# Grouped-query attention on one core: the order of all engines, planned by a search at build time, is replaced by an order written as a string

## The chip, the core and the metric

The kernel runs on one core of a Trainium2 chip. The metric is device time in microseconds (us) for one execution, the median of several. The core has five engines that each work through a list of instructions in order: TensorE (PE, matrix multiplication into PSUM), ScalarE (ACT), VectorE (DVE), GpSimd (POOL) and SyncE (SP, here only a queue of transfers). They wait for one another on semaphores. GpSimd works on SBUF alone; the scores lie in PSUM, where ScalarE and VectorE can read them.

## The reference: what is computed

```python
scores = scale * np.matmul(q_group, k_group.transpose(0, 1, 3, 2))
scores_max = np.max(scores, axis=-1, keepdims=True)
attn = np.exp(scores - scores_max)
attn = attn / (np.sum(attn, axis=-1, keepdims=True) + 1e-08)
output[:, q_start:q_end, :, :] = np.matmul(attn, v_group)
```

There are 8 batches, 8 query heads and 2 key/value heads (four query heads share one), 1024 positions and 64 values per head, in fp32. The scores are small, so the kernel leaves the maximum out: it takes exp(scale * score), multiplies by v with a column of ones appended, and divides by the sum that this column gives.

## The kernel before, in words

There are 64 jobs j, one for each batch and query head. A job has 8 tiles of scores ("pairs"), each 128 x 1024 in fp32, in one of three PSUM slots (`sp0` to `sp2`). A pair takes two score matmuls (L880) and then an exponential, in one of two ways:

- ScalarE: one ACTIVATE (L890) writes the pair as bf16 into `pt`.
- VectorE, by bit arithmetic: a "pass" (L901, `yt<-sp`) turns the scores into 16-bit integers whose bits are nearly those of a bf16 exponential. Two pairs make a chain, which takes three more steps in SBUF on 2048 columns: `zh` (L908, keeps the mantissa bits), `two` (L915, keeps the exponent bits, `et`) and `mul` (L924, `zt` = `yt` x `zt`). Both `et` and `zt` are then multiplied by v and added up in PSUM. The last four jobs add them on VectorE instead (L929).

GpSimd takes columns of `mul` off VectorE (L854). It does this in windows in which VectorE reads PSUM: the pass, the reciprocal of the sums (`rec`, L1007) and the normalization (`norm`, L1016). Each such multiplication is tied by a wait to the VectorE instruction just before the window.

TensorE multiplies by v in pieces of 128 rows (L942) into two PSUM banks; seven pieces fill a bank, which VectorE then normalizes into `ost`, from where SP stores it. The last job's pieces are done as its pairs become ready (L982). Dummy matmuls (L727) fill some of TensorE's idle time.

The inputs q, k and v are cast to bf16 by transfers that GpSimd issues into DRAM buffers, one for each tensor (L625); SP transposes, copies and stores.

The order of all this comes from `class Plan`, plain Python that runs when the kernel is built. It keeps a clock for each engine and advances the one that is earliest. Its constants (`M_...`) are durations in ns. For TensorE, `choices` says what could be next and which is preferred: `A` (scores for ScalarE), `D` (scores for VectorE), `V` (a few matmuls by v), `E` and `L` (pieces of the first and last job), `F` (a dummy), `W` (wait); `cost` plays each of them 7 us on and the best is taken. `quota` fixes how many pairs of a job go to VectorE. `dve` picks VectorE's next step by fixed keys. `gpsimd` is called as VectorE begins a window and gives one chain at most as many columns as fit: the window plus `M_GOVER` = 60 ns, in steps of 32 columns, at least 192. GpSimd's transfers are not in the plan: they are put behind multiplications afterwards, by the `room` that is left there. In the plan VectorE's steps take the same time whether or not GpSimd works beside them.

The plan's events, sorted by time, are then written out as instructions. From there each engine follows its list.

Of the kernel before, what the change touches and what calls it, by code (L numbers as in the profile page):

```python
# [10 lines left out]
M_START = 5450  # L11
# [6 lines left out]
M_FILL = 1e9  # L18
M_IDLE = 250
# [16 lines left out]
M_GP = 800  # L36
# [3 lines left out]
M_GOVER = 60  # L40
M_GLATE = 900
M_NORM = 531
M_HOLD = 1500
M_SPARE = 800
M_ISSUE = 900
M_LATE = 8500

M_GAP = 90
M_RUNWAY = 2100
M_BACK = 4100  # L50
M_WAIT = 250
M_TOL = 200

HORIZON = 7000
W_A = 1.0
W_D = 0.28
W_P = 0.02
W_LAG = 0
# [4 lines left out]
MXD = 2  # L63
MORE = 4
TAIL = 4
CHN = 2
SOON = 0
AHEAD = 3
LAST = ()
LONG = 6  # L70
FIRST = (2, 2, 1)
GWINS = 2
GFROM = 2
GTO = 5
GMIN = 192
GSTEP = 32
STEPS = (("zh", M_D4), ("two", M_D4), ("mul", M_D2), ("add", M_D2))


class Chain:  # L80
# [12 lines left out]
    def copy(self):  # L93
        c = Chain.__new__(Chain)
        c.__dict__.update(self.__dict__)
        c.pairs = self.pairs[:]
        return c

    def left(self):
        n = len(self.pairs)  # L100
        return sum(
            M_FIX + (self.share() if k == "mul" else 1024 * n) * r
            for k, r in STEPS[self.at : self.nsteps]
        )

    def share(self):

        return max(0, self.cols - 500 * max(0, GWINS - self.wins)) if self.nsteps == 3 else self.cols


class State:
    LISTS = "nxt dcount pcnt pmax a_of mms slot aq dq out norms lastp firstp twice".split()

    def copy(self):
        c = State.__new__(State)
        c.__dict__.update(self.__dict__)
        for k in self.LISTS:
            setattr(c, k, getattr(self, k)[:])
        new = {}

        def twin(ch):
            if ch is None:
                return None
            if ch.id not in new:
                new[ch.id] = ch.copy()
            return new[ch.id]

        c.chains = [twin(x) for x in self.chains]
        c.open = twin(self.open)
        c.heads = {k: v[:] for k, v in self.heads.items()}  # L130
        c.ev = None
        return c

    def note(self, *e):
        if self.ev is not None:
            self.ev.append(e)


class Plan:
# [5 lines left out]
    def __init__(self, nj, npt, nct, nyt):  # L145
# [9 lines left out]
        self.quota = [FIRST[j] if j < len(FIRST) else MXD + (j % MORE == MORE // 2) for j in range(nj)]  # L155
        self.quota[nj - len(LAST) :] = LAST
# [14 lines left out]
        s.tG = M_START + 9000  # L171
# [9 lines left out]
        s.ev = []  # L181
        self.run(s)
# [16 lines left out]
    def act(self, s):  # L199
        t = s.tA  # L200
        if not s.aq:
            s.tA = max(t, s.tP) + 1
        elif s.aq[0][0] > t:
            s.tA = s.aq[0][0]
        else:
            _, sl, j, c = s.aq.pop(0)
            s.note(t, "act", sl, j, c)
            s.idleA += t - s.endA
            s.tA = s.endA = t + M_ACT
            s.slot[sl] = s.tA + M_ATAIL + M_SEE  # L210
            self.ready(s, j, c, s.slot[sl])

    def gpsimd(self, s, t, window):


        at = max(t, s.tG)
        until = t + window + M_GOVER
        at += M_GLEAD
        for ch in s.chains:
# [7 lines left out]
            if ch.cols - w < GMIN:  # L227
                w = ch.cols
# [4 lines left out]
            s.note(t, "gmul", None, ch.id, (ch.cols, w))  # L233
            s.tG = at = at + M_GFIX + w * M_GCOL
            ch.parts += 1
            self.part(s, ch, s.tG + M_SEE + M_GLATE)
            break

    def dve(self, s):
        t, nj, end = s.tD, self.nj, None  # L240
        norm = s.norms and s.norms[0][0] <= t
        rec = norm and s.norms[0][1] == "rec"
        soon = s.dq and s.dq[0][0] <= t + (M_REC if rec else 0)
        if rec:
            _, _, lo, hi = s.norms[0]
            if soon:
                self.gpsimd(s, t, M_REC + 1134 + M_NORM)
                s.host = True
            s.note(t, "rec", (lo, hi), None, None)
# [3 lines left out]
        elif s.dq and s.dq[0][0] <= t and not (  # L253
            (norm and t - s.norms[0][0] > M_HOLD)
            or any(ch.pairs[0][0] < SOON for ch in s.chains)
        ):
# [15 lines left out]
            if not s.host:  # L272
                self.gpsimd(s, t, 1134 + (M_NORM if norm else 0))
            s.host = False
            s.follow = bool(norm)
            s.note(t, "dpass", sl, (ch.id, len(ch.pairs) - 1), (j, c))
# [3 lines left out]
            if len(ch.pairs) == (2 if j < LONG or j >= nj - 6 else CHN):  # L280
                s.chains.append(ch)
                s.open = None
        else:
            best = None
            if norm:
                late = s.dlast == s.norms[0][2]
                key = -1 if s.follow or s.norms[0][2] < NPIECE else 5 if late or s.dq else 0
                best = (late and key >= 0, key, None)
            for ch in s.chains:

                late = s.dlast == (ch.id, ch.at) and ch.at in (0, 3)
                first = (3, 4, 2, 1)[ch.at]
                if ch.at == 2 and ch.nsteps == 3 and ch.cols and ch.wins < GWINS:
                    if GFROM <= ch.pairs[0][0] < nj - GTO:
                        if s.dq and s.dq[0][0] < t + M_SPARE:
                            continue
                        first = 6
                key = (late, first, ch)
                if best is None or key[:2] < best[:2]:
                    best = key  # L300
            s.follow = False
            if best:
                at = max(t, s.dend + M_DEP) if best[0] else t
                ch = best[2]
                if ch is None:
                    _, _, lo, hi = s.norms.pop(0)
                    s.note(t, "norm", (lo, hi), None, None)
                    end = at + M_FIX + 64 * (hi - lo) * M_D1
                    s.out[self.group_of[lo] % 2] = end + M_DTAIL + M_SEE
                    s.dlast = None  # L310
                    s.end = s.pc == self.last and not s.left and not s.norms
                else:
                    n = len(ch.pairs)
                    kind, rate = STEPS[ch.at]
                    cols = ch.cols if kind == "mul" else 1024 * n
                    end = at
                    if cols:
                        s.note(t, kind, None, ch.id, n, cols)
                        end = at + M_FIX + cols * rate
                    if kind == "zh":  # L320
                        ch.zend = end + M_DTAIL + M_SEE
                    ch.at += 1
                    s.dlast = (ch.id, ch.at)
                    if ch.at == ch.nsteps:
                        s.chains.remove(ch)
                        self.part(s, ch, end + M_DTAIL + M_SEE)
        if end:
            s.idleD += t - s.endD
            s.tD = s.endD = end
            s.dend = end + M_DTAIL  # L330
        else:
            s.tD = max(t, s.tP) + 1
            for q in (s.dq, s.norms):
                if q:
                    s.tD = min(s.tD, q[0][0])
            s.tD = max(s.tD, t + 1)

    def pick_d(self, s):
        for j in range(s.a, min(self.nj, s.a + AHEAD)):
            if s.nxt[j] < 8 and s.dcount[j] < self.quota[j] and self.qready[j] <= s.tP:  # L340
                return j
        return None

    def choices(self, s):

        t, nj = s.tP, self.nj  # L350
        while s.a < nj and s.nxt[s.a] == 8:
            s.a += 1
        a = s.a
        cold = 2 if t < M_WARM else 1
        free = [x for x in (0, 1, 2) if s.slot[x] <= t]
        runway = s.tA - t + M_ACT * len(s.aq)
        slack = runway - cold * M_PAIR - M_PTAIL - (M_SWITCH if s.mode != "s" else 0)
        can_a = a < nj and len(s.aq) < 2 and self.qready[a] <= t and s.used_p < self.npt
        dj = None
        held = len(s.chains)  # L360
        if not s.dq and held < self.nyt and (s.open or s.used_c < self.nct):
            if max(s.tD - t, 0) + sum(ch.left() for ch in s.chains) < M_BACK:
                dj = self.pick_d(s)
        s.free, s.dj = free, dj
        can = []
        kind = None
        if free:
            can += ["A"] * can_a + ["D"] * (dj is not None)
            if dj is not None:
                if not can_a:  # L370
                    kind = "D"
                elif len(free) > 1 or slack <= M_GAP or s.mode == "s":
                    other = min(s.slot[x] for x in (0, 1, 2) if x != free[0])
                    late = not s.aq and other > s.tA - M_PAIR - M_PTAIL + M_TOL
                    kind = "A" if late or slack <= M_PAIR else "D"
# [679 lines left out]
```

## Time and profile before

The median of the three runs shown is 357.17 us (356.17 to 357.32). One execution was profiled.

| | |
|---|---|
| profiled execution | 356.55 us |
| its span, first to last instruction on the engines | 354.8 us |
| granted TensorE clock | 1.00 |
| ScalarE: exponentials (L890) | 372, 342.1 us busy |
| VectorE: passes (L901) | 140, 170.7 us |
| VectorE: `zh`, `two`, `mul` | 71 each; 47.9, 47.2 and 54.2 us |
| VectorE: `rec`, `norm` | 74 each; 73 of them 14.6 and 44.8 us |
| GpSimd: multiplications (L854) | 107, 131.9 us |
| GpSimd: transfers issued (L625) | 33 of q, 8 of k, 8 of v; 28.7 us |

In the costliest groups, "x" is the number of instructions, then come the engine's busy time in the group and the mean duration of one in ns, then the engine's idle time just before them and what ended most of it. Consecutive instructions of an engine overlap in the records, so a pass that lasts 1.22 us is followed by the next instruction after some 1.13. In the timeline a row begins with its start and its length in us.

### The profile page before, as it was taken

To read this page: it belongs to the slowest core of one execution; us is meant where nothing else is said; L and a number is where in the kernel's file an instruction comes from. 1 tells how busy PE (TensorE), PEld (TensorE's weight loads), DVE (VectorE), ACT (ScalarE), POOL (GpSimd) and SP (SyncE) were. 2 spreads that over 40 slices of the span, in tenths; PEclk is the share of its full clock that TensorE was granted. 3 is DMA by queue.
4 is the path that set the end of the run, shared out by engine and by line. 5 is a ranking of instruction groups with operands and counts; after the bars stand their busy time and mean duration, and the time that the engine had idled before them with its cause. 6 is when DMAs were issued, how large, how long until landed. Compare 5 with 4: busy or idle time off the path is not lost.

```text
span 354.8 us, 14070 instructions
## 1 busy us (share of the span) xinstructions
PE 346.3 (98%) x6236; PEld 223.1 (63%) x6236; DVE 345.3 (97%) x516; ACT 344.6 (97%) x376; POOL 160.6 (45%) x164
## 2 busy tenths in 40 slices
PE   8899999999999999999999999999999999999995
PEld 3556666666666666666666666666666666666665
DVE  4999999999999999999999999999999999999995
ACT  5999999999999999999999999999999999999993
POOL 3145554664355444563465645265543625570000
PEclk9999999999999999999999999999999999999999
DMA  6688555996675976496566976759675798556133
GB/s 159 123 134 160 127 106 124 132 151 126 131 137 117 135 141 120 84 181 157 105 95 133 164 136 132 137 84 173 135 93 124 119 174 125 122 91 126 29 91 120
DMA packets 96430, 44.82 MB, mean 126 GB/s; under 512 B 61153, under 2 KB 95073, under 8 KB 95585
## 3 DMA queue, kind: packets, MB, share of 16 engines
q1 hardware_dynamic: 94128, 31.48, 43.6%
q0 software_dynamic: 2096, 12.19, 23.9%
q8 instruction: 48, 0.79, 1.0%
q10 hardware_dynamic: 144, 0.26, 0.2%
q14 instruction: 14, 0.11, 0.1%
HBM read 27.13 MB, written 28.97 MB: 158 GB/s over the span
## 4 chain that ended last, share of the span: by engine, by line
ACT 70%; PE 24%; DVE 4%; issue 1%
ACT pt L890 70%; PE ops L942 12%; PE sp L880 10%; DVE yt L901 2%; PE ops L727 1%; DVE zt L924 1%; PE sp L982 1%; DVE zt L908 1%; DVE ost L1016 0%; DVE et L915 0%; PE sp L750 0%; PE ops L762 0%; PE ops L750 0%; DVE rec L1007 0%; DVE warm L619 0%
## 5 line engine op out<-in xcount | busy, mean ns | idle before, releaser
L890 ACT ACTIVATE pt<-sp 128x1024 bf16<-128x1024 f32 x372 | 342.1, 1039 | 0.7 <-PE sp L880 0.6
L854 POOL TENSOR_TENSOR zt<-yt,zt 128x448 bf16<-128x448 bf16 (+2 forms) x107 | 131.9, 1233 | 145.0 <-DVE et L915 45.3
L880 PE MATMUL sp<-qt,kt 64*128 64x512 bf16 x1024 | 172.7, 383 | 2.9 <-DVE yt L901 1.4
L942 PE MATMUL ops<-va,pt 128*128 128x65 bf16 x2872 | 175.3, 194 | 0.0
L901 DVE TENSOR_SCALAR yt<-sp 128x1024 uint16<-128x1024 f32 x140 | 170.7, 1219 | 0.8 <-PE sp L880 0.8
L942 PEld LDWEIGHTS <-pt 128*128 128x128 bf16 x2872 | 127.7, 97 | 33.4 <-issue 33.4
L942 PE MATMUL ops<-va,zt 128*128 128x65 bf16 x1096 | 127.7, 194 | 0.0
L942 PE MATMUL ops<-va,et 128*128 128x65 bf16 x1048 | 118.0, 194 | 0.0
L942 PEld LDWEIGHTS <-zt 128*128 128x128 bf16 x1096 | 87.5, 97 | 13.8 <-issue 13.1
L942 PEld LDWEIGHTS <-et 128*128 128x128 bf16 x1048 | 82.3, 98 | 17.6 <-issue 17.6
L880 PEld LDWEIGHTS <-kt 64*128 64x128 bf16 x1024 | 48.5, 93 | 55.9 <-issue 33.8
L924 DVE TENSOR_TENSOR zt<-yt,zt 128x896 bf16<-128x896 bf16 (+9 forms) x71 | 54.2, 763 | 0.0
L908 DVE TENSOR_SCALAR zt<-yt 128x2048 uint16<-128x2048 uint16 (+1 forms) x71 | 47.9, 675 | 0.2
L915 DVE TENSOR_SCALAR et<-yt 128x2048 uint16<-128x2048 uint16 (+1 forms) x71 | 47.2, 670 | 0.0
L1016 DVE TENSOR_TENSOR ost<-ops,rec 128x448 f32<-128x448 f32 (+2 forms) x73 | 44.8, 613 | 0.1
L625 POOL DMA_DIRECT2D qd<-in_q_dram x33 | 19.5, 592 | 4.8 <-PE sp L880 4.0
L1007 DVE RECIPROCAL rec<-ops 128x7 f32<-128x7 f32 (+2 forms) x73 | 14.6, 200 | 0.0
L727 PE MATMUL ops<-warm 128*128 128x128 bf16 (+1 forms) x36 | 5.7, 296 | 1.7 <-DVE warm L619 1.2
L625 POOL DMA_DIRECT2D kd<-in_k_dram x8 | 4.5, 560 | 5.0 <-PE sp L880 5.0
L727 PEld LDWEIGHTS <-warm 128*128 128x128 bf16 x36 | 2.8, 109 | 4.9 <-issue 3.7
L625 POOL DMA_DIRECT2D vd<-in_v_dram x8 | 4.7, 583 | 0.6 <-PE sp L880 0.6
L929 DVE TENSOR_TENSOR zt<-et,zt 128x2048 bf16<-128x2048 bf16 (+1 forms) x4 | 4.3, 1078 | 0.0
(38 smaller groups left out, 25.1 us busy)
## 6 DMA issues: line engine op xcount, KB each, us to landing
out_dram<-ost SPq DMA_DIRECT2D x64, 256.0 KB, 3.4
qd<-in_q_dram POOLq DMA_DIRECT2D x29, 256.0 KB, 4.8
kt<-kt SPq DMA_DIRECT2D x30, 64.0 KB, 3.6
va<-vd SPq DMA_DIRECT2D x30, 64.0 KB, 3.9
kd<-in_k_dram POOLq DMA_DIRECT2D x7, 256.0 KB, 4.2
vd<-in_v_dram POOLq DMA_DIRECT2D x7, 256.0 KB, 5.3
qt<-qd SPq DMA_TRANSPOSE x63, 4.0
qd<-in_q_dram POOLq DMA_DIRECT2D x5, 128.0 KB, 3.8
```

Source lines behind the costliest of these rows:

```text
L625: return nc.gpsimd.dma_start(out=t.rearrange("(a x) d -> a (x d)", a=128), in_=src.rearrange("(a x) d -> a (x d)", a=128),)
L727: nc.tensor.matmul(ops[bank][:, lo : lo + cols], lhsT=warm[:, 0:128], rhs=warm[:, 0:cols], start=not beside, stop=True, skip_group_check=b ...
L854: gps = nc.gpsimd.tensor_tensor(out=z, in0=flat(yt[j])[:, lo : lo + w], in1=z, op=ALU.mult)
L880: now = nc.tensor.matmul(sps[x][:, half, :], lhsT=t[lo : lo + D, c // NH, ci % NH * 128 : (ci % NH + 1) * 128], rhs=qt[j][lo : lo + D, 0, ...
L890: exps.append(nc.scalar.activation(out=p, in_=where_s[(j, c)], func=AF.Exp, scale=scale))
L901: vec = nc.vector.tensor_scalar(out=yt[ch][:, i, :, :], in0=where_s[c], scalar1=EXP_A, scalar2=EXP_B, op0=ALU.mult, op1=ALU.add,)
L908: vec = nc.vector.tensor_scalar(out=zt[j][:, 0:c], in0=yt[j][:, 0:c], scalar1=0x7F, scalar2=0x3F00, op0=ALU.bitwise_and, op1=ALU.bitwise_or,)
L915: vec = ins = nc.vector.tensor_scalar(out=et[j][:, 0:c], in0=yt[j][:, 0:c], scalar1=0x7F80, scalar2=None, op0=ALU.bitwise_and,)
L924: vec = nc.vector.tensor_tensor(out=z, in0=flat(yt[j])[:, 0 : cols[0]], in1=z, op=ALU.mult)
L942: nc.tensor.matmul(ops[plan.group_of[x] % 2][:, lo : lo + D + 1], lhsT=p[:, qs * 128 : (qs + 1) * 128], rhs=va[(b * G + h // HPG) % NVA][: ...
L1007: vec = nc.vector.reciprocal(out=to, in_=sums)
L1016: vec = nc.vector.tensor_tensor(out=to, in0=o, in1=by, op=ALU.mult)
```

## The change

`choices`, `cost`, `pick_d`, `quota`, the copies of the state and the keys by which `dve` chose are gone. In their place a string of letters, `ORDER`, is read one letter at a time, by whichever of TensorE and VectorE is next: for TensorE `A` and `a` to `d` (scores for ScalarE, and for VectorE from the job at hand or one of the three after it), `V`, `E`, `L`, `F`, `W` and `x` (close a chain of one pair); for VectorE `p` and `P` (a pass; with `P` the window given to GpSimd counts a normalization too), `r` and `R` (a reciprocal, in the same way), `n` (normalization), a digit (the next step of the chain with that number) and `i` (idle). The string was found by a search whose program is not part of the kernel.

`gpsimd` now runs its windows over by up to 100 ns instead of 60, in steps of 8 columns instead of 32, at least 96 at a time, and may serve several chains in one window. The plan lengthens a VectorE step in SBUF by what GpSimd runs into it beyond `M_GFREE` = 125 ns. Transfers of q (from job 10 on), k and v are in the plan: each has a due time and is placed before a window's multiplication where 850 ns are free, or ahead of it once it is 5 us overdue.

By the lists of instructions as built, this gives:

| | before | after |
|---|---|---|
| exponentials on ScalarE | 372 | 369 |
| passes on VectorE | 140 | 143 |
| `zh` and `two`, on 2048 / 1024 columns | 69 / 2 each | 71 / 1 each |
| `mul` on VectorE, columns | 71, 84,000 | 69, 67,520 |
| multiplications on GpSimd, columns | 107, 59,360 | 131, 78,912 |
| matmuls by v (L942) | 5016 | 5040 |

The core of the diff:

```diff
-M_GOVER = 60
+M_GOVER = 100
...
+M_GFREE = 125
+M_ISSUE = 850
+M_OVER = 5000
+NEED = 5150
...
-GMIN = 192
-GSTEP = 32
+GMIN = 96
+GREST = 64
+GSTEP = 8
...
+ORDER = """
+AaApFFFFFWFFAWWWWWWWWWWWWWWWWWWWWaWWWWWWWWWWApEEWWAW0WWWbWWWWApEEWWAWW0WWWaEpAEWWA0WWAFWWWWbFF0FE0AE
...
+VA0AVVVVVVVRVV0VVVVVVVVAanWWAVpVxVVVVVVVVVVAR0AWnWAVVV0VVVV0VVVVVL0LLLRnLLLLFFRFn
+"""
...
     def gpsimd(self, s, t, window):
+        while s.due:
+            x = max(s.tG, s.due[0][0])
+            if x + M_ISSUE > t + M_GLEAD:
+                if t - s.due[0][0] <= M_OVER:
+                    break
+                x = max(t, s.tG)
+            s.ev.append((x, s.due[0][1], None, s.due[0][2], None))
+            s.tG = x + M_ISSUE
+            s.due.pop(0)
...
-            if ch.cols - w < GMIN:
+            if ch.cols - w < GREST:
                 w = ch.cols
...
-            s.tG = at = at + M_GFIX + w * M_GCOL
+            s.tB = s.tG = at = at + M_GFIX + w * M_GCOL
             ch.parts += 1
             self.part(s, ch, s.tG + M_SEE + M_GLATE)
-            break
...
     def dve(self, s):
...
+            what = next(self.steps)
...
+            ch = s.chains[int(what)]
+            late = s.dlast == (ch.id, ch.at) and ch.at in (0, 3)
+            n = len(ch.pairs)
+            kind, rate = STEPS[ch.at]
+            cols = ch.cols if kind == "mul" else 1024 * n
+            end = at = max(t, s.dend + M_DEP) if late else t
+            if cols:
+                s.ev.append((t, kind, None, ch.id, n, cols))
+                end = at + M_FIX + cols * rate
+                end += max(0, s.tB - at - M_GFREE)
...
-    def choices(self, s):
...
     for when, kind, x, j, c, *cols in ev:
         if kind in ("ck", "cq", "cv"):
-            if gps is None:
-                begin(kind, j, True)
+            begin(kind, j, True)
+        elif kind in ("q", "k", "v"):
+            begin("c" + kind, j, False)
```

## The prediction

> **What bounds the kernel now.** I read the page's table of engines first, then the chain that ended last, then the costliest groups, and then the timeline of VectorE (DVE) and GpSimd (POOL) around single multiplications.
>
> ```profile
> PE 346.3 (98%) x6236; PEld 223.1 (63%) x6236; DVE 345.3 (97%) x516; ACT 344.6 (97%) x376; POOL 160.6 (45%) x164
> ACT 70%; PE 24%; DVE 4%; issue 1%
> L890 ACT ACTIVATE pt<-sp 128x1024 bf16<-128x1024 f32 x372 | 342.1, 1039 | 0.7 <-PE sp L880 0.6
> L854 POOL TENSOR_TENSOR zt<-yt,zt 128x448 bf16<-128x448 bf16 (+2 forms) x107 | 131.9, 1233 | 145.0 <-DVE et L915 45.3
> L901 DVE TENSOR_SCALAR yt<-sp 128x1024 uint16<-128x1024 f32 x140 | 170.7, 1219 | 0.8 <-PE sp L880 0.8
> L924 DVE TENSOR_TENSOR zt<-yt,zt 128x896 bf16<-128x896 bf16 (+9 forms) x71 | 54.2, 763 | 0.0
> ```
>
> ScalarE (ACT) and VectorE both stand still less than 1 us in front of their large groups: the work is divided between two full engines. The chain names ACT for 70%, but that is the tie being broken; VectorE has no more room. TensorE's 98% is a modelled figure, and its instructions wait in places, so I take it as not binding. GpSimd is idle half the time, but it may only multiply while VectorE reads PSUM (pass, reciprocal, normalization); where it runs over into VectorE's next SBUF step, the two meet. So the size of the change hangs on how a multiplication ends against that step. Three places of the timeline, VectorE's rows and then GpSimd's:
>
> ```profile
> 97.70 1.22 DVE L901 TENSOR_SCALAR yt<-sp 128x1024 uint16<-128x1024 f32 x1
> 99.36 0.69 DVE L908 TENSOR_SCALAR zt<-yt 128x2048 uint16<-128x2048 uint16 x1
> 99.96 0.69 DVE L915 TENSOR_SCALAR et<-yt 128x2048 uint16<-128x2048 uint16 x1
> 100.57 1.22 DVE L901 TENSOR_SCALAR yt<-sp 128x1024 uint16<-128x1024 f32 x1
> ...
> 97.96 1.52 POOL L854 TENSOR_TENSOR zt<-yt,zt 128x704 bf16<-128x704 bf16 x1 [3.25 <-DVE et L915]
> 100.74 1.03 POOL L854 TENSOR_TENSOR zt<-yt,zt 128x448 bf16<-128x448 bf16 x1 [1.25 <-DVE et L915]
> ```
>
> ```profile
> 73.62 0.21 DVE L1007 RECIPROCAL rec<-ops 128x7 f32<-128x7 f32 x1
> 75.36 0.73 DVE L908 TENSOR_SCALAR zt<-yt 128x2048 uint16<-128x2048 uint16 x1
> 76.01 1.21 DVE L901 TENSOR_SCALAR yt<-sp 128x1024 uint16<-128x1024 f32 x1
> ...
> 73.90 1.63 POOL L854 TENSOR_TENSOR zt<-yt,zt 128x768 bf16<-128x768 bf16 x1 [0.85 <-DVE rec L1007]
> ```
>
> Two things are to be seen. First, the run-over: at 99.36 the multiplication still ran until 99.48, 0.12 into the step, and the next instruction came 0.60 after it, as at 99.96 to 100.57 with no multiplication beside it. At 75.36 it ran until 75.53, 0.17 into the step, and the next came after 0.65. So about 0.125 us is free and what goes beyond is paid one for one. Second, the lead: the multiplication at 100.74 began 0.17 after its pass, the ones at 97.96 and 73.90 began 0.26 and 0.28 after theirs. In the instruction lists the late ones are those that wait on TensorE as well (for the reuse of the zt buffer), which takes GpSimd a separate wait instruction: 51 of 107 before, 56 of 131 in the changed kernel.
>
> **ScalarE's part.** The lists have 369 exponentials for 372. At 342.1/372 = 0.92 us each that is -2.76. Behind the last one (ends 348.62) the kernel of before still runs 3.02 us, because TensorE has 64 matmuls of an older piece and all 64 of the last one to do:
>
> ```profile
> 347.76 0.69 DVE L929 TENSOR_TENSOR zt<-et,zt 128x1024 bf16<-128x1024 bf16 x1
> ...
> 350.71 0.21 DVE L1007 RECIPROCAL rec<-sp 128x8 f32<-128x8 f32 x1 [1.03 <-PE sp L982]
> 350.95 0.69 DVE L1016 TENSOR_TENSOR ost<-sp,rec 128x512 f32<-128x512 f32 x1
> ```
>
> In the changed order only 8 matmuls of about 0.03 us stand behind the last exponential's data: 0.05 + 0.25, then 0.24 + 0.69 for the last two VectorE instructions, 1.25 in all, so -1.8. ScalarE alone would allow -4.5; it is not what decides.
>
> **VectorE's part, removed and added.** Start to start, a pass takes 1.13 (100.57 to the reciprocal at 101.70), a step on 2048 columns 0.60, one on 1024 columns 0.34. Three more passes: +3.40. Two more full and one fewer half of each of the two bit steps: 2 x (2 x 0.60 - 0.34) = +1.72. VectorE's own multiplications shrink from 84,000 columns in 71 instructions to 67,520 in 69; the slope between the 896 and the 2048 column forms (0.611 and 1.222 us) is 0.53 ns a column: -8.74, and -0.13 for two starts. Sum -3.75. Reciprocals and normalizations stay at 74 each.
>
> **What GpSimd gives back.** It takes 78,912 columns in 131 multiplications for 59,360 in 107. From 1.031 us for 448 columns and 1.514 for 704 (1.89 ns a column), 464 take 1.061, 752 take 1.605, 800 take 1.695. The stretches that cover them are as long as before: pass alone 1.13; pass and normalization 1.66 (97.70 to 99.36); reciprocal, pass and normalization 1.74 (73.62 to 75.36). With the short lead of 0.17 the run-overs are 0.10, 0.115 and 0.125: free. With the long lead they are 0.19, 0.205 and 0.22, of which 0.065, 0.08 and 0.095 are paid. The lists put 10, 14 and 17 such multiplications in front of an SBUF step: 0.65 + 1.12 + 1.62 = +3.4. By the same count the old kernel pays about 0.03 on seven of 768 columns, 0.2. So +3.2, on an engine without slack: whatever is behind the held step moves, the pass first, then the PSUM slot that it frees, then the score matmuls and the exponential that wait for it in TensorE's fixed order. Bounds for it: 0 (if these delays fall on steps that would have waited) and 5 (long leads of 0.28 and free room of 0.10).
>
> Here the Trainium skill speaks against the change. "SBUF — State Buffer", in "SBUF: two separate sides", says that VectorE and GpSimd hold the shared port pair exclusively for a whole instruction and that the loser is fully blocked. By that rule every run-over costs its whole length: about 59 short-lead ones of 0.10 to 0.125 (6.3) and 41 long-lead ones (8.5), with 0.7 behind reciprocals some 15.5 us; the old kernel would pay 7.4 by the same count. The increase would be 8.1 in place of 3.2. The row at 99.36 (0.12 of overlap, no delay) decides for 3.2.
>
> **VectorE's end.** In the old kernel 3.88 us lie between the start of its last addition (347.76) and the end (351.64). In the changed order TensorE needs that addition's result only for the last but one of its eight groups; from the addition's start it is 0.6 + 0.13 + 0.5 of matmuls + 0.95, 2.2 in all: -1.7. One normalization (0.53) moves from behind the addition to ahead of it: +0.53. VectorE's path: -3.75 + 3.2 - 1.7 + 0.53 = -1.7.
>
> **TensorE, transfers, queues.** 24 more matmuls at 0.03 are 0.7 us under the two full engines; if that cover were gone they would be the price. Half as many dummy matmuls go. The 41 transfers issued by GpSimd in the new order stand directly behind a multiplication, as most did before. The same page warns that such a transfer starves while VectorE runs a two-port step; the trace has 0.55 us beside a multiplication of VectorE and 0.73 beside a bit step:
>
> ```profile
> 104.07 0.55 POOL L625 DMA_DIRECT2D kd<-in_k_dram  x1
> 106.75 0.73 POOL L625 DMA_DIRECT2D qd<-in_q_dram  x1
> ```
>
> In both orders at least two steps of VectorE, 0.9 us or more, lie between that place and the next pass, so I take 0; a transfer that came late would push the next multiplication out by at most 0.3, six such in the whole run 2 us. They start up to some us earlier or later than before, but every transfer into DRAM has a buffer of its own and lands in about 5 us, while the rules start it 16 to 25 us ahead of its head. SP's queue keeps its rules for transposes, copies and stores; nothing is moved past them beyond the heads' own times: 0.
>
> **Sum.** ScalarE would allow -4.5, VectorE -1.7; the later one sets the end. The profiled execution took 356.55 (span 354.8 and 1.75 around it): 354.85. The median of the runs shown is 357.17, which gives 355.5. I take 355.4. A measurement of this kernel can tell about 0.3% (1.07 us) from no change.
>
> **Rivals.** (1) The delays are absorbed: VectorE's held steps are those that would have waited, or the instructions behind them wait anyway. Then both engines gain about what was taken off: -3.75 - 1.2 for VectorE, -4.5 for ScalarE less new small waits; about -3.6, 353.6. For it: passes are often ready well before VectorE takes them. Against: 345.3 of 354.8 busy. Chance 0.24. (2) The longer multiplications eat the gain: long leads at 0.28, more waits of ScalarE because fewer exponentials stand ready; 5 instead of 3.2 gives +0.1, about 357. Chance 0.21. (3) Slower: the free room of 0.125 does not hold where the multiplications run to its edge in nearly every stretch. At a free room of 0.09 the 41 long-lead ones cost 4.8 and the 59 short ones 0.9; from there it is slower by over 0.3%, and with none (the page's rule) it ends 4.9 later than forecast, at 360.3. Chance 0.09. That the change does nothing is excluded: the instruction lists differ on every engine.
>
> **How the numbers follow.** My forecast, a gain of 1.1 to 2.7 us (354.5 to 356.1), has 0.46. Faster by over 0.3% is that and rival 1: 0.70. Within 0.3% is rival 2: 0.21. Slower: 0.09. The range reaches from rival 1 (353.2) to the upper part of rival 2 (357.5).
>
> **What would show it.** Right: 369 exponentials, VectorE's multiplications about 10 us less, GpSimd near 173 us busy; bit steps and multiplications behind a long-lead one last 0.75 to 0.78 instead of 0.69, with VectorE still without idle time and some idle time in front of the exponentials; a tail of about 1.3 us behind the last exponential. Wrong: ScalarE still without idle time (rival 1), steps behind short-lead multiplications stretched too (rival 3), or transfers that hold up a multiplication.

## The result and the profile after

The changed kernel took 354.69 us (median of four runs, 354.56 to 354.93) against 357.21 for the kernel before (356.17 to 357.32): a ratio of 0.9937, with a 95% interval of 0.9918 to 0.9956. That is 2.5 us faster. The forecast was 355.4 in a range of 353.2 to 357.5, "faster" with 0.70.

The page of the changed kernel: engines, the chain that ended last, and the costliest groups that answer to those shown before (the lines of the program moved: 890 is now 764, 854 is 732, 901 is 775, 908 is 782, 915 is 789, 924 is 798, 929 is 803, 982 is 856, 1007 is 881, 1016 is 890; each experiment's edit moves them again).

```profile
PE 344.6 (98%) x6247; PEld 223.8 (63%) x6247; DVE 344.3 (98%) x519; ACT 344.3 (98%) x373; POOL 204.1 (58%) x188
DVE 67%; PE 21%; ACT 8%; issue 3%; DVEq 0%
L764 ACT ACTIVATE pt<-sp 128x1024 bf16<-128x1024 f32 x369 | 341.8, 1034 | 0.5 <-PE sp L754 0.4
L732 POOL TENSOR_TENSOR zt<-yt,zt 128x464 bf16<-128x464 bf16 (+5 forms) x131 | 173.4, 1324 | 107.7 <-DVE et L789 35.5
L775 DVE TENSOR_SCALAR yt<-sp 128x1024 uint16<-128x1024 f32 x143 | 172.6, 1207 | 0.6 <-PE sp L754 0.5
L782 DVE TENSOR_SCALAR zt<-yt 128x2048 uint16<-128x2048 uint16 x72 | 50.1, 696 | 0.1
L798 DVE TENSOR_TENSOR zt<-yt,zt 128x832 bf16<-128x832 bf16 (+7 forms) x69 | 45.1, 654 | 0.0
```

GpSimd is 41.5 us busier with multiplications (173.4 for 131.9), VectorE's own take 9.1 less (45.1 for 54.2). The chain went over from ScalarE (70%) to VectorE (67%). That alone is no proof that VectorE decides; the forecast's claim that it does rests on e3, e4 and e7 below. ScalarE's busy time is only 0.3 us less although three exponentials are gone: more of them start late, so their records overlap less. The distances from one start to the next that exceed 0.93 us add up to 4.8 us above 0.917 where they added up to 2.3. The page doesn't show that as idle time, because a record lasts 1.03 us and so covers a start that comes up to 0.11 late.

Two places of the timeline show what decides, first VectorE's rows and then GpSimd's, in two stretches of the changed kernel that have the same steps (reciprocal, pass, normalization, bit step):

```profile
289.85 0.19 DVE L881 RECIPROCAL rec<-ops 128x7 f32<-128x7 f32 x1
291.58 0.77 DVE L782 TENSOR_SCALAR zt<-yt 128x2048 uint16<-128x2048 uint16 x1
292.28 0.68 DVE L789 TENSOR_SCALAR et<-yt 128x2048 uint16<-128x2048 uint16 x1
...
290.11 1.69 POOL L732 TENSOR_TENSOR zt<-yt,zt 128x800 bf16<-128x800 bf16 x1 [0.76 <-PE sp L754]
```

```profile
308.69 0.19 DVE L881 RECIPROCAL rec<-ops 128x7 f32<-128x7 f32 x1
310.43 0.68 DVE L782 TENSOR_SCALAR zt<-yt 128x2048 uint16<-128x2048 uint16 x1
311.03 1.21 DVE L775 TENSOR_SCALAR yt<-sp 128x1024 uint16<-128x1024 f32 x1
...
308.85 1.70 POOL L732 TENSOR_TENSOR zt<-yt,zt 128x800 bf16<-128x800 bf16 x1 [0.63 <-DVE et L789]
```

In the first, the multiplication waits on TensorE too, by a separate wait instruction just before it, and starts 0.26 after the reciprocal; it ends at 291.80, 0.22 into the bit step, which lasts 0.77, and the next instruction comes 0.70 after it. In the second it starts 0.16 after the reciprocal and ends at 310.55, 0.12 into the step; the step lasts 0.68 and the next comes after 0.60. I added up for every SBUF step of VectorE how far a multiplication ran into it beyond 0.125 us, and call the sum the paid run-over: 2.80 us on 44 steps here, 0.30 on 10 in the kernel before. Of the 2.80, 2.76 lie behind the multiplications that wait on TensorE: these 56 start 0.253 us (median) after the VectorE instruction that opens their stretch, the other 75 start 0.158 after it.

The tail of the changed kernel, VectorE and then TensorE:

```profile
347.08 0.69 DVE L803 TENSOR_TENSOR zt<-et,zt 128x1024 bf16<-128x1024 bf16 x1
348.90 0.21 DVE L881 RECIPROCAL rec<-sp 128x8 f32<-128x8 f32 x1 [0.42 <-PE sp L856]
349.14 0.69 DVE L890 TENSOR_TENSOR ost<-sp,rec 128x512 f32<-128x512 f32 x1
...
346.70 1.66 PE L856 MATMUL sp<-va,pt 128*128 128x65 bf16 x48
348.20 0.41 PE L856 MATMUL sp<-va,zt 128*128 128x65 bf16 x8
348.45 0.41 PE L856 MATMUL sp<-va,pt 128*128 128x65 bf16 x8
```

VectorE ends at 349.83 where it ended at 351.64: 1.81 earlier. The profiled executions took 354.69 and 356.55, so 1.86 less. The medians differ by more, 2.5, because the kernel before was profiled in one of its better executions. In later measurements its executions ranged from 355.7 to 360.7 around medians of 356.95 to 357.19, the twelve longest at a granted clock of 0.987 to 0.995; of e4's 22 one took 717.87 us, unexplained, and is left out of its ratio.

### The profile page after: what moved, and what is told of

Read it like the earlier page. It is cut to its first block, busy times and chain, and to the rows that moved or that the text cites. A ratio compares the mean times of both kernels' runs of the same rounds, so it can differ in the third digit from the quotient of the medians.

```text
span 352.9 us, 14128 instructions
## 1 busy us (share of the span) xinstructions
PE 344.6 (98%) x6247; PEld 223.8 (63%) x6247; DVE 344.3 (98%) x519; ACT 344.3 (98%) x373; POOL 204.1 (58%) x188
## 4 chain that ended last, share of the span: by engine, by line
DVE 67%; PE 21%; ACT 8%; issue 3%; DVEq 0%
DVE yt L775 35%; PE ops L816 10%; DVE et L789 8%; PE sp L754 8%; ACT pt L764 8%; DVE zt L798 7%; DVE ost L890 7%; DVE zt L782 7%; DVE rec L881 2%; PE ops L619 1%; PE sp L856 1%; PE sp L642 0%; DVE kt L663 0%; PE ops L654 0%; PE ops L642 0%
## 5 line engine op out<-in xcount | busy, mean ns | idle before, releaser
L732 POOL TENSOR_TENSOR zt<-yt,zt 128x464 bf16<-128x464 bf16 (+5 forms) x131 | 173.4, 1324 | 107.7 <-DVE et L789 35.5
L775 DVE TENSOR_SCALAR yt<-sp 128x1024 uint16<-128x1024 f32 x143 | 172.6, 1207 | 0.6 <-PE sp L754 0.5
L816 PE MATMUL ops<-va,zt 128*128 128x65 bf16 x1120 | 130.9, 194 | 0.0
L816 PE MATMUL ops<-va,et 128*128 128x65 bf16 x1072 | 121.7, 194 | 0.0
L816 PEld LDWEIGHTS <-zt 128*128 128x128 bf16 x1120 | 89.9, 97 | 12.3 <-issue 12.1
L816 PEld LDWEIGHTS <-et 128*128 128x128 bf16 x1072 | 84.2, 98 | 20.6 <-issue 20.6
L782 DVE TENSOR_SCALAR zt<-yt 128x2048 uint16<-128x2048 uint16 x72 | 50.1, 696 | 0.1
L789 DVE TENSOR_SCALAR et<-yt 128x2048 uint16<-128x2048 uint16 x72 | 49.6, 691 | 0.0
L798 DVE TENSOR_TENSOR zt<-yt,zt 128x832 bf16<-128x832 bf16 (+7 forms) x69 | 45.1, 654 | 0.0
```

The source lines that it names most:

```text
L732: gps = nc.gpsimd.tensor_tensor(out=z, in0=flat(yt[j])[:, lo : lo + w], in1=z, op=ALU.mult)
L775: vec = nc.vector.tensor_scalar(out=yt[ch][:, i, :, :], in0=where_s[c], scalar1=EXP_A, scalar2=EXP_B, op0=ALU.mult, op1=ALU.add,)
L782: vec = nc.vector.tensor_scalar(out=zt[j][:, 0:c], in0=yt[j][:, 0:c], scalar1=0x7F, scalar2=0x3F00, op0=ALU.bitwise_and, op1=ALU.bitwise_or,)
L789: vec = ins = nc.vector.tensor_scalar(out=et[j][:, 0:c], in0=yt[j][:, 0:c], scalar1=0x7F80, scalar2=None, op0=ALU.bitwise_and,)
L798: vec = nc.vector.tensor_tensor(out=z, in0=flat(yt[j])[:, 0 : cols[0]], in1=z, op=ALU.mult)
L816: nc.tensor.matmul(ops[plan.group_of[x] % 2][:, lo : lo + D + 1], lhsT=p[:, qs * 128 : (qs + 1) * 128], rhs=va[(b * G + h // HPG) % NVA][: ...
```

## The experiments

Ratios are to the kernel before, measured in the same session. e1 to e4 ran in one session and e5 to e8 in another, in which the kernel before took 357.09 and 357.19. Where two traces are compared, the time runs from the start of the first exponential to VectorE's end; over the traces that start varies between 5.8 and 6.5 us.

Theory: GpSimd's longer multiplications take work off VectorE, and give back what runs over into VectorE's next SBUF step beyond 0.125 us; that is paid where the multiplication had to wait on TensorE as well and so starts 0.09 us later, and VectorE passes it on to the end. Rivals: the delays are absorbed, and the exponentials taken from ScalarE decide; or every run-over is paid.

**e1: the changed kernel again**, as the base of e2 to e4.

> The changed kernel once more, as the base of its neighbours. Every theory: 354.7 us, 2.5 below the kernel before.

Measured: 354.62 (ratio to the kernel before 0.9921, 0.9893 to 0.9949). Paid run-over in its trace: 2.65 us.

**e2: the wait on TensorE ahead of time.** A small instruction of GpSimd takes the wait for the reuse of the buffer off the multiplication. `lastread` and `lastgp` hold the last matmul and the last GpSimd multiplication on a buffer; the lines that fill them are left out here.

```diff
...
             zt[j] = zp.tile([128, CHN, 2, HS], U16, name="zt")
+            zorder.append(j)
+            old = zorder[-1 - NCT] if len(zorder) > NCT else None
+            if old in lastread and old in lastgp:
+                tiny = nc.gpsimd.memset(spot, 0.0)
+                tc.add_manual_dep(tiny.ins, lastread[old].ins.name, Sync, reason="buffer read")
+                tc.add_manual_dep(tiny.ins, lastgp[old].ins.name, Sync, reason="buffer written")
...
```

> The order is kept; for each reused zt buffer GpSimd gets a 1-column memset of a spare tile right behind the bit step that opens the buffer, and the wait on TensorE is put on this memset, so that 53 of the 56 long-lead multiplications wait on VectorE alone. Theory (the paid run-over of the long-lead multiplications, 2.8 us in the trace of the changed kernel, reaches the end one for one): leads of 0.165 instead of 0.255, no step of VectorE stretched, 354.7 - 2.8 = 351.9, at the least 352.6 if ScalarE takes over. Rival A (the delays are absorbed in waits, the exponentials decide): 354.7. Rival B (the memsets stand in GpSimd's way): above 354.7.

Measured: 353.36 (ratio 0.9886, 0.9853 to 0.9919), 1.3 below e1 and not 2.8. The paid run-over fell to 0.11 us, so the early wait does take it away; but of 2.54 us only 1.3 reached the end in the medians, 1.5 in the traces. The late starts of the exponentials fell from 4.8 to 3.2. The chain went back to ScalarE:

```profile
ACT 87%; PE 11%; issue 1%; DVE 0%
```

**e3: long-lead multiplications shorter by 48 columns.** The columns go back to VectorE; the order is kept. A new helper, not shown, changes the planned widths: of a chain's first multiplication by the first number, of its second by the second.

```diff
...
+    plan.ev = resized(plan.ev, -48, 0)
     ev = list(plan.ev)
```

> 54 of the long-lead multiplications of GpSimd (the first of their chain) get 48 columns less, VectorE's multiplications of these chains 48 more (2,592 columns in all). Theory: 48 columns are 0.09 us, so nearly all of the paid 2.8 us goes, and VectorE's own work grows by 2,592 x 0.52 ns = 1.35: 354.7 - 2.7 + 1.35 = 353.3. Rival A (delays absorbed): between 354.7 and 356.0.

Measured: 353.84 (0.9901, 0.9864 to 0.9938), 0.8 below e1. The traces have 342.56 for 343.59: 1.03 less. The paid run-over fell from 2.65 to 0.25, which is 2.40, and 2,592 columns cost 1.35; that leaves 1.05. VectorE does more work itself and the kernel is faster.

**e4: the same multiplications longer by 48 columns.**

```diff
+    plan.ev = resized(plan.ev, 48, 0)
```

> The same 54 multiplications get 48 columns more, VectorE's 2,592 fewer. Theory: 44 of them already run past the free room and pay 0.09 more each (4.0), about 10 behind a reciprocal begin to pay 0.03 each (0.3), VectorE saves 1.35: 354.7 + 2.95 = 357.6. Rival A (delays absorbed): 353.3 to 354.7.

Measured: 356.97 (0.9991, 0.9976 to 1.0006), 2.35 above e1. The paid run-over is 6.37 us on 55 steps, 3.72 more; less the 1.35 that VectorE saves, 2.37. In the traces it is 2.28. (The expectation had put the increase at 4.3, so it came out 0.6 too high.) VectorE's bit step with a multiplication of 848 columns, and that multiplication:

```profile
293.69 0.86 DVE L815 TENSOR_SCALAR zt<-yt 128x2048 uint16<-128x2048 uint16 x1
294.47 0.68 DVE L822 TENSOR_SCALAR et<-yt 128x2048 uint16<-128x2048 uint16 x1
...
292.21 1.78 POOL L765 TENSOR_TENSOR zt<-yt,zt 128x848 bf16<-128x848 bf16 x1 [0.73 <-DVE rec L914]
```

It ran until 293.99, 0.30 into the step, and the next instruction came 0.78 after the step's start. With 0.12, 0.22 and 0.30 of run-over the distance to the next instruction is 0.60, 0.70 and 0.78: beyond 0.12 it grows one for one. The 492 full bit steps with a run-over in eight traces (before, after, e1, e3, e4, e5, e7, e8) say the same: up to 0.125 us the median distance is 0.599, and above, a straight line through the 248 distances has a slope of 0.99 and leaves 0.599 at 0.126. 48 columns too many eat the whole gain of the change.

**e5: e2 with a no-op in place of the memset.** The question was whether the memset itself cost something.

```diff
-                tiny = nc.gpsimd.memset(spot, 0.0)
+                tiny = nc.gpsimd.engine_nop()
```

> As e2_early_wait, but the early wait on TensorE is carried by an engine no-op of GpSimd, which touches no memory, in place of the memset. In e2 the paid run-over fell from 2.65 to 0.11 us and VectorE's end came only 1.5 earlier; bit steps with a memset beside them (overlap 0.11 to 0.125, free otherwise) were 0.02 to 0.04 longer. Theory 1 (the memset's own port use took part of the gain, the rest went where ScalarE became the bound): 0.3 to 0.6 below e2, 352.8 to 353.1. Theory 2 (ScalarE alone limits e2): as e2, 353.4.

Measured: 353.29 (0.9888, 0.9872 to 0.9904): as e2, so the memset itself had cost nothing that reaches the end. The bit steps beside the place of the memset are back at 0.60 to the next, which moved nothing.

**e6: the early wait in the kernel before.** The edit is that of e5, made in the kernel before.

> The kernel before with the same early wait on no-ops (51 of 107 multiplications wait on TensorE; 46 lose it). Its multiplications are shorter, and it paid 0.3 us of run-over in its trace. Theory (the long lead costs only where the window is filled to the edge): 0 to 0.3 below the kernel before. Rival (a wait on TensorE costs the kernel by itself, whatever the length): 1 us or more below it.

Measured: 356.91 for 357.19 (0.9993, 0.9976 to 1.001): no difference that can be told, as the theory has it. The wait on TensorE costs only where the stretch is filled to its edge, which the old widths (448, 704 and seven of 768) hardly did: the paid run-over was 0.30 us and is 0.00 here. Its profiled execution showed something else: TensorE waited for the transposed q of the fourth job (view of waits, columns: engine and line, what it waited for, total us, times, longest).

```profile
PE sp L882 <- DMA qt<-qd: 1.8, 1, 1.8
```

**e7: short-lead multiplications shorter by 48 columns**, the counterpart of e3.

```diff
+    plan.ev = resized(plan.ev, 0, -48)
```

> The counterpart of e3_long_less: 47 short-lead multiplications (the second of their chain) get 48 columns less, VectorE's 2,256 more. Theory: these run over within the free room, so nothing is won: 2,256 x 0.52 ns = 1.17 us more on VectorE, 354.6 + 1.1 = 355.7. Rival (any run-over is paid, as the page on SBUF has it): 47 x 0.09 = 4.2 less, 351.6 to 354.6.

Measured: 355.88 (0.9961, 0.9946 to 0.9976), 1.26 above e1, 1.07 in the traces; 1.17 was the price of the columns. A run-over of 0.09 to 0.12 costs nothing, so taking it away wins nothing. The same edit on the other half of the multiplications made the kernel faster: this pair speaks against both rivals at once. It also shows how little the chain that ended last says between two engines that are both full: here it names ScalarE for most of the span, and yet the work added to VectorE reached the end.

```profile
ACT 59%; PE 20%; DVE 18%; issue 2%; DVEq 0%
```

**e8: the transfers by the old rule.** The changed order, with q, k and v placed as before the change (behind a multiplication with 0.9 us of room).

```diff
+    ev = [e for e in plan.ev if e[1] not in ("q", "k", "v")]
...
+            for _, what, _, who, _ in then.get(nth, []):
+                begin(what, who, False)
+            nth += 1
```

> The changed kernel with the transfers of q, k and v placed by the old rule (behind a multiplication with 0.9 us of room), nothing else changed. If their new place is worth nothing: 354.6, within 0.5. If the longer multiplications leave the old rule no room and transfers push multiplications out: up to 2 us above.

Measured: 354.90 (0.9932, 0.9916 to 0.9948), 0.3 above e1, within the spread of that; in the traces 343.67 for 343.59. The new placement of the transfers is worth nothing that can be measured.

**e9: the fourth job's q earlier, in the kernel before.**

```diff
     cast_q(2)
+    cast_q(3)
...
-        if j == 3 or (j > 3 and j % 2 == 0) or j == NJ - 1:
+        if (j > 3 and j % 2 == 0) or j == NJ - 1:
```

> The kernel before, with the transfer of the fourth job's q issued right behind the third's (2.9 us into the span) instead of behind the copy of v (6.7 to 6.9 us). In the trace of e6_before_nop TensorE's first score matmul of that job waited 1.8 us for its transposed q and the kernel stayed 0.97 us behind; the profiled execution of the kernel before did not wait. The changed order needs this job's scores later (two more pairs of its neighbours stand ahead). Theory (the wait strikes the kernel before in many executions, and the changed order gained its absence): the median falls by 0.4 to 0.9, to 356.2 to 356.7, and spreads less. Rival (the spread of the kernel before has another cause): 357.1, unchanged.

Measured: 356.75 for 357.12 (0.9987, 0.997 to 1.0005). The middle half of the runs lies within 0.5 us (356.5 to 357.0) where that of the kernel before lies within 1.1 (356.5 to 357.7). That is what the theory wants in direction, but the interval includes no change: inconclusive.

**e10 (in spite of its name, e5 once more) and e11 (e5 with the earlier q).** The edit of e11 is that of e9.

> e5_early_nop again, on the same chip as its neighbour e11, as its base: 353.3.

> e5_early_nop with the same early transfer of the fourth job's q. No run of the changed order's kin showed that wait, so nothing is to be won: 353.3 within 0.4; if the wait also strikes it unseen, 352.5 to 352.9.

Measured: 353.07 (0.9871, 0.9835 to 0.9906) and 353.48 (0.9881, 0.9846 to 0.9917). Nothing is won, and in the traces of the changed order TensorE never waits for a transposed q.

**e12: less work for VectorE in e5.** 64 columns of each of VectorE's multiplications are left out, so these columns of the exponential stay unfinished.

```diff
-            z = flat(zt[j])[:, 0 : cols[0]]
+            short = cols[0] - 64
+            z = flat(zt[j])[:, 0:short]
...
-                out=z, in0=flat(yt[j])[:, 0 : cols[0]], in1=z, op=ALU.mult
+                out=z, in0=flat(yt[j])[:, 0:short], in1=z, op=ALU.mult
```

> e5_early_nop with 64 columns left out of each of VectorE's 69 multiplications (those columns of zt stay unmultiplied, so this part of the exponential is left out): 69 x 64 x 0.52 ns = 2.3 us less on VectorE, nothing else changed. Theory (with the long leads gone ScalarE is the bound, and only part of the paid run-over could reach the end for that reason): 353.2, at most 0.4 less. Rival (VectorE is still the bound, and the rest of the 2.5 us was lost on VectorE itself): 351.0.

Measured: 353.19 (0.9883, 0.9853 to 0.9912), as e5. VectorE's multiplications, in e5 and then in e12:

```profile
L806 DVE TENSOR_TENSOR zt<-yt,zt 128x832 bf16<-128x832 bf16 (+7 forms) x69 | 45.1, 654 | 0.0
```

```profile
L807 DVE TENSOR_TENSOR zt<-yt,zt 128x768 bf16<-128x768 bf16 (+7 forms) x69 | 42.7, 619 | 0.0
```

2.4 us less on VectorE and 0.1 at the end in the medians (0.3 in the traces): with the run-over gone VectorE's work is not the bound any more. That is why e2 and e5 won 1.3 and not 2.5. What bounds them instead was not tested. The chain points to ScalarE's exponentials (87%) and TensorE, which feeds them in a fixed order (11%), and the exponentials' late starts still add up to 3.0 us in e5; but no run took work from either engine. e5 is the fastest kernel: 353.3 and 353.1 in two measurements, 1.3 below the changed kernel.

## Why the prediction was right, step by step

- **ScalarE's part.** Three exponentials fewer, but the last one ended at 348.12, only 0.50 earlier than 348.62: the late starts grew by 2.5 us, and in e2 they shrank with the run-over. That ScalarE alone doesn't decide was right; the bound of -4.5 was never near. The tail behind the last exponential is 1.71 us and not 1.25, and the idle time that was to show in front of the exponentials doesn't (0.5 us for 0.7), since it hides in the overlap of the records.
- **VectorE's part and what GpSimd gives back.** Widths, counts and stretches were as built. The paid run-over was put at 3.4 us on 41 multiplications; it measured 2.80 on 44 steps (2.65 in e1), 40 of them behind late multiplications, in part because these started at 0.253 in the median and not at 0.26 to 0.28. The old kernel's 0.2 was 0.30. With the measured sizes VectorE's way to the last addition is -3.75 + 2.80 - 0.30 + 0.53 = -0.72. The addition starts at 347.08 for 347.76, -0.68, but that close agreement is chance: 0.25 of it is an earlier first exponential (6.22 for 6.47), which varies as much between executions of one kernel. From the first exponential on it is -0.43, so 0.29 us are not accounted for. That the run-over passes to the end one for one, as long as VectorE is the bound, was shown by e3 and e4.
- **The rule that the Trainium skill states** ("SBUF — State Buffer", in "SBUF: two separate sides": the shared port pair is held for a whole instruction, and the other engine is fully blocked), applied to the whole run-over as the records show it, would have made the change slower. That failed against the row at 99.36 in the old trace, and again in e7 and in the row at 310.43: overlaps up to 0.12 us cost nothing. Beyond that the delay is one for one, as the rule has it. So it isn't shown that both engines use the port at once during the free 0.125 us. VectorE's own records overlap by 0.08 us (0.68 long, 0.60 apart), so a record is longer than what holds up the next instruction; the free room may be a matter of where records begin and end.
- **VectorE's end** was the mis-sized term. I had 2.2 us from the start of the last addition to the end, with only 16 matmuls behind its result. It is 2.75: in the new trace all 64 last matmuls run in one piece from 346.70, because TensorE had only just finished the piece before. TensorE's own work of 2 us sets the tail: the addition's result is ready at 347.77 and TensorE takes it at 348.20, and VectorE then waits 0.42 for TensorE. The tail shrank by 1.13 and not by 1.7. This error and the one on the run-over (0.6 the other way, with the 0.1 for the old kernel) nearly cancel: -1.81 for -1.7 in the profiled executions, -1.56 from the first exponential on. That the sum came out so near is luck; its direction and the main term are not.
- **From the profiled execution to the median.** The forecast of 355.4 leaned on both 354.85 (profiled) and 355.5 (median). The changed kernel's profiled execution lies on its median, that of the kernel before 0.6 below its own. So about 0.6 of the 2.5 us is a difference in the typical execution that the profiled one of the kernel before doesn't show, and the forecast had no term for it. A part may lie outside the engines' span: in 13 of 85 later executions of the kernel before 2.2 to 2.9 us lay there instead of 1.8, in none of e1's seven. Inside the span a wait for the fourth job's q is a candidate (e6 showed it, 0.98 us behind from there on; the changed order takes that job's scores later), but e9 didn't settle it: this part stays open.
- **Transfers at 0**: right, by e8.
- **Rivals.** Rival 1 (absorbed) fell with e3, e4 and e7, rival 3 with e7; rival 2 would have needed longer leads than there were, and e4 shows how near it was: 48 columns.

## What to carry to other kernels

Where the steps of two engines hold each other up, ask of each piece of work not how long it is but where its end falls against the next step of the other engine, and what can make its start late: here 0.09 us of lead on 56 of 131 multiplications cost VectorE most of 2.8 us. An instruction that has to wait on two engines can have one of the waits taken by an earlier instruction of its own queue that has nothing else to do. When two engines are both full, a saving on one counts only up to the slack of the other: 2.5 us taken off VectorE were worth 1.3, and the next 2.4 next to nothing.

## What I had not expected of the hardware

A GpSimd multiplication that waits on TensorE besides VectorE has a separate wait instruction in front of it in these traces, and starts 0.09 us later (0.253 for 0.158 in the median), within a narrow spread. In 53 of the 56 it waits on GpSimd itself too; the three without that wait start as late (0.22 to 0.25). 60 engine no-ops, which take these waits earlier for 53 multiplications, cost nothing that shows. VectorE's distance to the next instruction grows one for one with the recorded run-over beyond about 0.125 us, with no cost below. A memset of one column beside a bit step (e2) made the distance mostly 0.02 to 0.04 us longer where a multiplication ran over by 0.10 to 0.125 us (11 steps: 0.627 in the median, for 0.599 without a memset).
